# Key and value projections of an RWKV-7/GLA decoder trunk in plain float32, with the first group's scores and inversion placed later

## The chip, the cores and the metric

The kernel runs on one core of one Trainium2 chip. The metric is the device time of one execution in microseconds (us), median of several runs, lower is better. The engines are named as in the profile: PE (TensorE, matmuls; PEld is its weight load), DVE (VectorE), ACT (ScalarE), POOL (GpSimd) and SP, whose queue issues every DMA of this kernel.

## The reference

A two-layer decoder trunk on 272 tokens (16 learned meta tokens and 256 tokens of one sequence), width 2048, float32. Layer 0 mixes tokens by RWKV-7, layer 1 by gated linear attention; each is followed by a squared-ReLU MLP of width 8192. The change lies in layer 0:

```python
xx = jnp.pad(x, ((0, 0), (1, 0), (0, 0)))[:, :-1] - x
xr, xw, xk, xv, xa, xg = (x + xx * mix[i] for i in range(6))
r = xr @ w_rkv[0]
k = xk @ w_rkv[1]
v = xv @ w_rkv[2]
...
kk = hs(k * k_k)
kk = kk / jnp.maximum(jnp.sqrt(jnp.sum(kk * kk, axis=-1, keepdims=True)), 1e-12)
k = k * (1.0 + (a - 1.0) * k_a)
...
def step(S, inp):                     # 32 heads of 64
    r_t, w_t, k_t, v_t, a_t, b_t = inp
    sa = jnp.einsum('bhvk,bhk->bhv', S, a_t)
    S = S * w_t[:, :, None, :] + sa[..., None] * b_t[:, :, None, :] + v_t[..., None] * k_t[:, :, None, :]
    y = jnp.einsum('bhvk,bhk->bhv', S, r_t)
```

## The kernel before

Activations lie transposed: features on the 128 partitions, 272 tokens along the free dimension, so a vector of width 2048 is 16 tiles. A weight matrix is read in pieces of 128 x 1024 (512 KB, eight blocks of 128 x 128), two pieces for one output tile of 128 features.

**Products.** Most projections go through `proj`. `wload` loads a piece into one of three buffers `raw`, ScalarE rounds it into `hi` (L134) and VectorE forms the rest `lo = raw - hi` (L135), both of the type fp32r and with two buffers each. `mm3` then issues three matmuls for a block: hi by the high part of x (L140), hi by its low part (L141), lo by its high part (L142). The mixed inputs are split in the same way by `hl`. `proj32` is the other form: it loads a piece into `raw` and multiplies it as it is, in float32, with one matmul a block (L195), x being float32 too (`mix32`). Before the change it serves the three small projections (decay, learning rate, gate) alone.

**RWKV layer.** After the receptance projection comes the key stage, a loop over 16 output tiles f ("columns" here). A column projects k, in a PSUM bank of the ring `pj` for even f and of the ring `pt` for odd f (two banks each), loads `ca` (the decay sum and the learning rate, written earlier) by DMA, and forms on ScalarE and VectorE the scaled vectors `bk` and `ar`, which go to DRAM (`bkd`, `ard`). Two small matmuls per column sum over heads: L465 needs `sq`, L480 needs `kn`. At f = 3 the value input xv is mixed, at f = 4 the vectors of the first four columns (group 0 of four, eight heads each) are loaded back as BK and AR. At f = 6 all five token chunks of group 0 get their scores: `scores(0, c)` fills two `pt` banks with eight matmuls (L416) which VectorE evicts under a mask into AM. Then `invert(0)` is made: a generator of 52 steps on VectorE (transposes L431, L434, L445, L449, and 30 update pairs `upd`, `sysA`) that inverts the triangular 32 x 32 systems. From f = 8 on seven of its steps are issued per column.

The recurrence follows, group by group (g = 0 to 3), chunk by chunk (c = 0 to 4): `state` (L592) needs S of the chunk before, `solve` (L604), `emit`, which writes the new S on VectorE, `inner`, `turn`. Here the order on TensorE is written by hand: between the dependent steps `R(n)` runs n steps of a list of other products, one step being one 128 x 128 block. The list begins with the value projection (`v_proj`, 16 tiles of 16 blocks, 256 steps) and goes on with the output projection. 52 steps run before `merge(0)` (L535, L545), the counts in GAPS run inside the chunks, MARK gives the count reached before the merge of the next group (134, 214, 286). The scores and the inversion of group g+1 run inside group g; each merge waits for its inversion. `ahead` loads the next weight piece.

Elsewhere a scheduler of the language decides the order on each engine; DMA loads of weights have a raised priority. SP, like each engine, works its own list in order.

Of the kernel before, what the change touches and what calls it, by code (L numbers as in the profile page):

```python
# [17 lines left out]
P = 128  # L18
D = 2048
KT = D // P  # L20
NMETA = 16
SEQ = 256
T = NMETA + SEQ
# [30 lines left out]
class Kern:  # L54
# [130 lines left out]

    def proj32(self, srcs, x, n):
        nc = self.nc
        ps = self.pj()
        for i, s in enumerate(srcs):
            with self.tc.high_priority(offset=2000):  # L190
                raw = self.t(self.wp, [P, 1024], "raw", self.raw_bufs)
                nc.sync.dma_start(raw, s)
            for j in range(8):
                kt = 8 * i + j
                nc.tensor.matmul(ps[:, :n], raw[:, j * P : (j + 1) * P], x(kt), start=kt == 0, stop=kt == 8 * len(srcs) - 1)  # L195
        return ps[:, :n]
# [69 lines left out]
    def rwkv(self, done):  # L266
# [111 lines left out]
        for f in range(NR + 2, KT):  # L378
            nc.scalar.copy(rr[f], self.proj(pair(wr, f), xr, T))
            if f == NR + 2:  # L380
                for i in range(2):
                    nc.scalar.activation(gs[i], self.proj32(pair(lw, 2 + i), xg, T), AF.Sigmoid)
                xk = mix(2, ep)
            for i in range(3 if f < 14 else 2):
                lora(3 * (f - 10) + i if f < 14 else 12 + 2 * (f - 14) + i)
# [66 lines left out]
        for f in range(KT):  # L452
            r = rr[f]
            bk, ar = st2[0][f % 2], st2[1][f % 2]
            ps = self.proj(pair(wk, f), xk, T, bank=self.ptr if f % 2 else None)
            ca = self.t(ep, [P, 2, T], "ca", 2)
# [26 lines left out]
            if f == 3:  # L483
                xv = mix(3, self.xp)
                early2.close()
# [7 lines left out]
            if f == 4:  # L493
                load(0)
            if f == 6:
                for c in range(5):
                    scores(0, c)
                inv = invert(0)
            if f > 7:
                for _ in range(7):  # L500
                    next(inv, None)
# [171 lines left out]
        def units(x, n, ps):  # L673
            for i in range(n):
                hi, lo = weights.pop(0)
                for j in range(8):
# [4 lines left out]
                    if kt < 8 * n - 1:  # L681
                        yield

        def v_proj(f):
            ps = self.pj()[:, :T]
            yield from units(xv, 2, ps)
            nc.scalar.copy(hres[:, f], ps)
            tt(rr[f], rr[f], hres[:, f])
            yield
# [36 lines left out]
        def ahead():  # L726
            if srcs:
                weights.append(self.wload(srcs.pop(0)))
# [344 lines left out]
```

## Time and profile before

| | |
|---|---|
| three runs, median (lowest to highest) | 2659.4 us (2648.26 to 2670.31) |
| profiled execution | 2651.93 us, span 2649.9 us, mean granted clock 0.986 |
| instructions in the span | 47706 |
| PE, PEld | 96%, 89% busy |
| DVE, ACT, POOL | 64%, 47%, 0% busy |
| DMA | 450.17 MB, mean 170 GB/s |
| chain that ended last | 77% PE, 3% DVE, 1% ACT |
| key stage in the trace | about 167 to 332 us, up to the first merge |
| recurrence up to the merge of group 3 | about 332 to 582 us |

A busy PE is not a PE at its peak: a matmul shows about 0.29 us where the next one starts 0.125 us later. So prices of matmuls are read here from the starts of neighbouring rows. Rows name the line, engine, operation and the tiles written and read; `[1.86 <-ACT sq L462]` at the end of a row is the idle time before it and what ended it.

### The profile page before, as it was taken

How to read it: one execution, taken by the hardware profiler on the slowest of the kernel's cores; microseconds unless marked ns; L12 is line 12 of the kernel's file. 1: busy time of each engine (PE TensorE's matmuls, PEld its weight loads, DVE VectorE, ACT ScalarE, POOL GpSimd, SP SyncE). 2: the span in 40 equal slices, each digit the busy share in tenths (PEclk: the TensorE clock that was granted, in tenths of full speed). 3: DMA queues.
4: the chain of work that ended last, by engine and by line, in shares of the span. 5: the costliest groups of instructions: out<-in, count | busy, mean ns of one | idle time of the engine just before them, and what ended most of it. 6: DMA issues, size and time to landing. Idle time of an engine off the chain costs nothing.

```text
span 2649.9 us, 47706 instructions
## 1 busy us (share of the span) xinstructions
PE 2551.9 (96%) x19492; PEld 2364.2 (89%) x19492; DVE 1688.0 (64%) x2794; ACT 1257.3 (47%) x2011; POOL 10.8 (0%) x35
## 2 busy tenths in 40 slices
PE   7998988888999999999999999999999999999998
PEld 7887977777999999999999999998888888888887
DVE  8677976775755545545545666676766656656665
ACT  5364644445544434434434544454555535435444
POOL 0000000000000000000000000000000000000000
PEclk9998999989999999999999999999999999999999
DMA  5565732322455555555555544444555555555554
GB/s 192 180 217 205 245 137 85 100 79 93 160 174 176 175 175 175 176 176 178 177 177 176 176 150 148 155 167 144 188 186 189 186 189 189 186 189 189 186 190 159
DMA packets 137083, 450.17 MB, mean 170 GB/s; under 512 B 15760, under 2 KB 23696, under 8 KB 136864
## 3 DMA queue, kind: packets, MB, share of 16 engines
q1 hardware_dynamic: 136864, 447.12, 49.3%
q8 instruction: 153, 2.51, 0.4%
q14 instruction: 66, 0.54, 0.1%
HBM read 431.07 MB, written 15.99 MB: 169 GB/s over the span
## 4 chain that ended last, share of the span: by engine, by line
PE 77%; DVE 3%; ACT 1%; issue 0%; DVEq 0%; ACTq 0%
PE pj L168 23%; PE pj L140 13%; PE pj L142 13%; PE pj L141 13%; PE pj L169 12%; DVE lo L135 1%; PE pt L908 1%; PE pm L657 0%; PE pu L917 0%; DVE upd L268 0%; PE pt L897 0%; DVE sysA L268 0%; PE pm L648 0%; PE pm L558 0%; PE pt L416 0%
## 5 line engine op out<-in xcount | busy, mean ns | idle before, releaser
L134 ACT CAST hi<-raw 128x1024 fp32r<-128x1024 f32 (+1 forms) x834 | 813.6, 983 | 1086.7 <-PE pj L141 566.8
L135 DVE TENSOR_TENSOR lo<-raw,hi 128x1024 fp32r<-128x1024 f32 (+1 forms) x834 | 946.8, 1142 | 596.6 <-ACT hi L134 583.6
L140 PE MATMUL pj<-x,hi 128*128 128x272 f32 x2224 | 657.0, 296 | 6.6 <-ACT x L308 4.1
L142 PE MATMUL pj<-x,lo 128*128 128x272 f32 x2224 | 645.1, 290 | 0.2 <-DVE lo L135 0.2
L141 PE MATMUL pj<-x,hi 128*128 128x272 f32 x2224 | 643.4, 289 | 0.0
L168 PE MATMUL pj<-x,hi 128*128 128x512 f32 x1664 | 587.6, 396 | 0.6 <-DVE x L827 0.6
L169 PE MATMUL pj<-x,lo 128*128 128x256 f32 x1664 | 468.6, 282 | 1.3 <-DVE lo L135 1.3
L140 PEld LDWEIGHTS pj<-x,hi 128*128 128x128 f32 x2224 | 421.4, 190 | 15.1 <-ACT x L308 4.9
L141 PEld LDWEIGHTS pj<-x,hi 128*128 128x128 f32 x2224 | 424.2, 191 | 2.0
L142 PEld LDWEIGHTS pj<-x,lo 128*128 128x128 f32 x2224 | 420.7, 189 | 1.6 <-DVE lo L135 0.7
L168 PEld LDWEIGHTS pj<-x,hi 128*128 128x128 f32 x1664 | 313.2, 188 | 76.3 <-issue 2.9
L168 PE MATMUL pj<-h,hi 128*128 128x512 f32 x1024 | 358.5, 394 | 0.0
L169 PEld LDWEIGHTS pj<-x,lo 128*128 128x128 f32 x1664 | 314.1, 189 | 2.8 <-DVE lo L135 1.9
L140 PE MATMUL pj<-h,hi 128*128 128x272 f32 x1024 | 294.7, 288 | 0.0
L142 PE MATMUL pj<-h,lo 128*128 128x272 f32 x1024 | 293.9, 287 | 0.0
L141 PE MATMUL pj<-h,hi 128*128 128x272 f32 x1024 | 293.5, 287 | 0.0
L169 PE MATMUL pj<-h,lo 128*128 128x256 f32 x1024 | 288.5, 282 | 0.0
L168 PEld LDWEIGHTS pj<-h,hi 128*128 128x128 f32 x1024 | 192.4, 188 | 44.3
L141 PEld LDWEIGHTS pj<-h,hi 128*128 128x128 f32 x1024 | 193.7, 189 | 0.0
L169 PEld LDWEIGHTS pj<-h,lo 128*128 128x128 f32 x1024 | 193.5, 189 | 0.0
L140 PEld LDWEIGHTS pj<-h,hi 128*128 128x128 f32 x1024 | 192.6, 188 | 0.0
L142 PEld LDWEIGHTS pj<-h,lo 128*128 128x128 f32 x1024 | 192.1, 188 | 0.0
(246 smaller groups left out, 2223.1 us busy)
## 6 DMA issues: line engine op xcount, KB each, us to landing
raw<-mlp_w_d SPq DMA_DIRECT2D x512, 512.0 KB, 3.2
raw<-gla_in_d SPq DMA_DIRECT2D x98, 512.0 KB, 3.2
raw<-w_rkv_d SPq DMA_DIRECT2D x80, 512.0 KB, 3.7
raw<-gla_o_d SPq DMA_DIRECT2D x32, 512.0 KB, 3.2
raw<-w_r_d SPq DMA_DIRECT2D x16, 512.0 KB, 3.3
raw<-rw_oA_d SPq DMA_DIRECT2D x16, 512.0 KB, 3.3
raw<-rw_oB_d SPq DMA_DIRECT2D x16, 512.0 KB, 3.2
ard<-ar SPq DMA_DIRECT2D x16, 288.0 KB, 3.7
```

The lines of the kernel that those rows point to most:

```text
L134: nc.scalar.copy(hi[:, h], raw[:, h])
L135: nc.vector.tensor_tensor(out=lo[:, h], in0=raw[:, h], in1=hi[:, h].bitcast(F32), op=ALU.subtract)
L140: nc.tensor.matmul(out, hi[:, ws], xh, start=first, stop=False)
L141: nc.tensor.matmul(out, hi[:, ws], xl, start=False, stop=False)
L142: nc.tensor.matmul(out, lo[:, ws], xh, start=False, stop=last)
L168: nc.tensor.matmul(wide, hi[:, ws], x[kt][:, :, off : off + SEQ], start=kt == 0, stop=False)
L169: nc.tensor.matmul(ps[:, :SEQ], lo[:, ws], x[kt][:, 0, off : off + SEQ], start=False, stop=kt == nk - 1)
L908: nc.tensor.matmul(pa[:w, i * C : (i + 1) * C], KX[i][:, dt, s * P : s * P + w], Q[:, dt, i * C : (i + 1) * C], start=dt == 0, stop=dt == 1)
```

## The change

The key projection and the value projection use plain float32: xk and xv are mixed without a split, k goes through `proj32`, which gets the argument `bank`, and `v_proj` multiplies raw pieces itself, `ahead` loading the 32 pieces of the value weights without the split. The output projection stays as it was. Of group 0, chunk c of the scores is issued at column 6 + c instead of all five at column 6; the inversion is made at column 10, and its steps are issued eleven per column from column 11 on, instead of seven from column 8. Lines up to L494 keep their numbers; the value matmul is L693 afterwards, its load L739.

```diff
-    def proj32(self, srcs, x, n):
+    def proj32(self, srcs, x, n, bank=None):
         nc = self.nc
-        ps = self.pj()
+        ps = bank() if bank else self.pj()
...
-                xk = mix(2, ep)
+                xk = mix32(2, ep)
...
-            ps = self.proj(pair(wk, f), xk, T, bank=self.ptr if f % 2 else None)
+            ps = self.proj32(pair(wk, f), xk, T, bank=self.ptr if f % 2 else None)
...
-                xv = mix(3, self.xp)
+                xv = mix32(3, self.xp)
...
-            if f == 6:
-                for c in range(5):
-                    scores(0, c)
+            if 5 < f < 11:
+                scores(0, f - 6)
+            if f == 10:
                 inv = invert(0)
-            if f > 7:
-                for _ in range(7):
+            if f > 10:
+                for _ in range(11):
                     next(inv, None)
...
         def v_proj(f):
             ps = self.pj()[:, :T]
-            yield from units(xv, 2, ps)
+            for i in range(2):
+                w = weights.pop(0)
+                for j in range(8):
+                    if j == 3:
+                        ahead()
+                    kt = 8 * i + j
+                    nc.tensor.matmul(ps, w[:, j * P : (j + 1) * P], xv(kt), start=kt == 0, stop=kt == KT - 1)
+                    if kt < KT - 1:
+                        yield
...
         def ahead():
-            if srcs:
+            if len(srcs) > len(order) - 4 - KT:
+                with tc.high_priority(offset=2000):
+                    raw = self.t(self.wp, [P, 1024], "raw", self.raw_bufs)
+                    nc.sync.dma_start(raw, srcs.pop(0))
+                weights.append(raw)
+            elif srcs:
                 weights.append(self.wload(srcs.pop(0)))
```

How the scheduler moves instructions, at three places. First TensorE where the scores of group 0 begin; `pj_2391` is k of column 6, `pt_2546` of column 7, the other `pt` tiles are score banks. Before:

```order
L142 MATMUL pj_2391<-x_1151,lo_2425 128x272
L465 MATMUL pm_2463<-sq_2456,cst_117 128x272
L416 MATMUL pt_2486<-AR_433_2194,BK_432_2193 128x128
L416 MATMUL pt_2487<-AR_433_2194,BK_432_2193 128x128
...
L416 MATMUL pt_2534<-AR_433_2194,BK_432_2193 64x64 x4
L416 MATMUL pt_2535<-AR_433_2194,BK_432_2193 64x64 x4
L140 MATMUL pt_2546<-x_1136,hi_2549 128x272
```

and now, with `pj_2039` k of column 6, `pt_2106` of column 7, `kn_2010` of column 5 and `kn_2065` of column 6:

```order
L195 MATMUL pj_2039<-x_1143,raw_2050 128x272 x2
L416 MATMUL pt_2094<-AR_369_1922,BK_368_1921 128x128 x4
L416 MATMUL pt_2095<-AR_369_1922,BK_368_1921 128x128 x4
L195 MATMUL pt_2106<-x_1136,raw_2107 128x272 x2
L195 MATMUL pt_2106<-x_1137,raw_2107 128x272 x2
L480 MATMUL pm_2035<-kn_2010,cst_117 128x272
L465 MATMUL pm_2071<-sq_2064,cst_117 128x272
L195 MATMUL pt_2106<-x_1138,raw_2107 128x272 x2
```

Where all five chunks stood between columns 6 and 7, one chunk stands there now, and L480 of column 5 comes behind it.

Second, VectorE during the inversion: `sysA` and `upd` are its steps, `lo` a split of a weight piece, `kn`, `kk`, `bk`, `ar` the vectors of a column. Before (column 8):

```order
L135 TENSOR_TENSOR lo_2778<-raw_2775,hi_2777 128x1024
L268 TENSOR_TENSOR kn_2707<-pj_2641,kn_2707 128x272
L268 TENSOR_TENSOR upd_2959<-sysA_2197 128x184
L268 TENSOR_TENSOR bk_1719<-kn_2707,iW_2704 128x4x64
L268 TENSOR_TENSOR bk_1719<-kn_2707,iW_2704 128x16
L469 SCALAR_TENSOR_TENSOR kk_2705<-sq_2706,kk_2705 128x272
L476 SCALAR_TENSOR_TENSOR kn_2707<-r_15_89,vecs_119,kn_2707 128x272
```

and now (column 11):

```order
L268 TENSOR_TENSOR sysA_1925<-sysA_1925,upd_2517 128x23x8
L268 TENSOR_TENSOR kn_2400<-pt_2374,kn_2400 128x272
L268 TENSOR_TENSOR upd_2520<-sysA_1925 128x198
L268 TENSOR_TENSOR bk_1664<-kn_2400,iW_2397 128x4x64
L268 TENSOR_TENSOR bk_1664<-kn_2400,iW_2397 128x16
L268 TENSOR_TENSOR sysA_1925<-sysA_1925,upd_2520 128x22x9
L476 SCALAR_TENSOR_TENSOR kn_2400<-r_18_92,vecs_119,kn_2400 128x272
L268 TENSOR_TENSOR upd_2523<-sysA_1925 128x210
```

The splits are gone, and a step of the inversion stands between most instructions of a column.

Third, SP at the weight loads of column 7 and the loads of `ca`. Before (`raw_2547` and `raw_2577` are the pieces of column 7, `ca_2357` is column 5's):

```order
L478 DMA ard_80<-ar_1722 128x576
L475 DMA bkd_79<-bk_1720 128x576
L457 DMA ca_2357<-cad_78 128x544
L128 DMA raw_2547<-w_rkv_d 128x1024
L401 DMA BK_432_2193<-bkd_79 128x4x576
L128 DMA raw_2577<-w_rkv_d 128x1024
```

and now (`raw_2107` and `raw_2117` are the pieces of column 7, `ca_2005` is column 5's, `ca_2060` column 6's):

```order
L475 DMA bkd_79<-bk_1663 128x576
L401 DMA BK_368_1921<-bkd_79 128x4x576
L192 DMA raw_2107<-w_rkv_d 128x1024
L192 DMA raw_2117<-w_rkv_d 128x1024
L457 DMA ca_2005<-cad_78 128x544
L457 DMA ca_2060<-cad_78 128x544
```

The load of column 5's `ca` stood ahead of both pieces of column 7 and stands behind them now.

## The prediction

> **What bounds the kernel now.** I read the page's busy table first, then the busy time by stage, then the waits of the stages that the change touches, and last single rows of TensorE for prices. The line of busy times:
>
> ```profile
> PE 2551.9 (96%) x19492; PEld 2364.2 (89%) x19492; DVE 1688.0 (64%) x2794; ACT 1257.3 (47%) x2011; POOL 10.8 (0%) x35
> ```
>
> TensorE sets the pace of the whole, but the change touches only the stretch from the key projection to the third merge of the recurrence. Busy time there by stage; the columns are the stage, its length, busy us of PE, PEld, DVE, ACT and POOL with their instructions, granted clock, DMA share and GB/s:
>
> ```profile
> 167.00:332.00 165.00, 151.85 (x1079) 141.56 (x1080) 145.08 (x386) 97.78 (x193) 2.06 (x3) 0.94 0.68 228
> 332.00:409.00 77.00, 65.26 (x1004) 59.70 (x1000) 58.19 (x134) 31.84 (x72) 1.63 (x3) 0.93 0.38 129
> 409.00:494.00 85.00, 73.51 (x1022) 64.34 (x1016) 62.82 (x144) 37.43 (x85) 1.63 (x3) 0.94 0.30 100
> 494.00:582.00 88.00, 70.71 (x1006) 61.64 (x1008) 67.44 (x157) 38.38 (x89) 1.63 (x3) 0.93 0.26 82
> ```
>
> The first row holds the 16 columns of the key projection and 52 steps of the value projection, the other three the recurrence of groups 0 to 2 up to the merge of the next. TensorE is idle for 13.1, 11.7, 11.5 and 17.3 us, 53.7 us in all, and a clock of 0.93 or 0.94 over 415 us is worth another 27 us. So about 80 us are lost there, and a change that adds TensorE work can be paid from them. What TensorE waits for (us in all, times, longest), in the key stage:
>
> ```profile
> PE pm L465 <- ACT sq L462: 4.3, 5, 1.9
> PE pm L480 <- DVE kn L476: 3.1, 4, 1.4
> PE pt L416 <- DMA AR<-ard: 2.8, 1, 2.8
> PE pt L416 <- DVE AM L268: 2.6, 4, 1.1
> ```
>
> in group 0:
>
> ```profile
> PE pu L592 <- DVE upd L268: 5.0, 1, 5.0
> PE pu L592 <- DVE S L268: 4.5, 2, 3.3
> ```
>
> in group 1:
>
> ```profile
> PE pu L592 <- DVE S L268: 5.0, 2, 2.8
> PE pm L648 <- DVE hres L658: 3.3, 2, 2.4
> ```
>
> and in group 2:
>
> ```profile
> PE pt L535 <- DVE sysA L445: 6.5, 2, 6.3
> PE pu L592 <- DVE S L268: 4.2, 2, 2.9
> ```
>
> All but the AR load end on VectorE or ScalarE, the two engines that the change relieves.
>
> **Price of one weight block.** TensorE just before, in and just after the gate projections, which are plain float32 already; the columns are start and duration in us:
>
> ```profile
> 75.73 0.29 PE L140 MATMUL pj<-x,hi 128*128 128x272 f32 x1
> ...
> 79.87 14.83 PE L195 MATMUL pj<-x,raw 128*128 128x272 f32 x64
> 94.33 0.49 PE L140 MATMUL pj<-x,hi 128*128 128x272 f32 x1
> ```
>
> From 75.73 to the L195 row stand 33 matmuls of the three-product form: (79.87-75.73)/33 = 0.1255 us each, 0.376 us for the three of one 128x128 block. The 64 records of L195 are two output tiles of 16 blocks, two records a block: (94.33-79.87)/32 = 0.452 us. A block costs 0.0755 us more in plain float32. The Trainium skill ("FP8 and Floating Point Precision", TensorE Precision Notes) says that true FP32 takes four passes through the array; at the 0.1255 us of a pass here that would be 0.502 us a block and +64 us over the 512 blocks. The L195 row decides against the size, not the sign: it is 0.452, and the sum goes by that.
>
> **Key projection, 16 columns of 16 blocks.** Grouped rows of the stretch 167 to 332 (count, then busy us, mean ns and idle time before):
>
> ```profile
> L140 PE MATMUL pj<-x,hi 128*128 128x272 f32 x178 | 52.6, 295 | 0.0
> L140 PE MATMUL pt<-x,hi 128*128 128x272 f32 x128 | 38.9, 304 | 0.0
> L135 DVE TENSOR_TENSOR lo<-raw,hi 128x1024 fp32r<-128x1024 f32 (+1 forms) x47 | 48.2, 1040 | 5.2 <-ACT hi L134 5.0
> L268 DVE TENSOR_TENSOR x<-xm,x 128x272 fp32r<-128x272 f32 x10 | 4.2, 431 | 0.3 <-ACT x L308 0.2
> L268 DVE TENSOR_TENSOR upd<-sysA 128x30 f32<-128x30 f32 (+14 forms) x30 | 9.8, 327 | 0.3
> L268 DVE TENSOR_TENSOR sysA<-sysA,upd 128x30 f32<-128x30 f32 (+14 forms) x30 | 9.8, 327 | 0.3
> L449 DVE STREAM_TRANSPOSE AM<-sysA 32x256 f32<-32x256 f32 x8 | 4.7, 622 | 0.1
> L431 DVE STREAM_TRANSPOSE sysA<-AM 32x256 f32<-32x256 f32 x8 | 4.4, 594 | 0.1
> L445 DVE STREAM_TRANSPOSE sysA<-sysA 32x256 f32<-32x256 f32 x4 | 2.4, 646 | 0.1
> ```
>
> 178+128 = 306 blocks (key, and the first of value) gain 0.0755 us: **+23.1 us**. VectorE loses 48.2 + 4.2 of its 145.1 us, and ScalarE the cast hi<-raw that stands ahead of each lo. So the two small waits of a column (L465 for sq, L480 for kn) should shrink. The casts of the mixed inputs go too; those of xk stood beside TensorE work before 167 and I cost them at nothing; were that cover gone it would be a gain of 16 x 0.431 = 6.9 us of VectorE.
>
> The lump of the first group's scores is what can be won back. TensorE around it:
>
> ```profile
> 218.10 0.29 PE L142 MATMUL pj<-x,lo 128*128 128x272 f32 x1
> 220.24 0.73 PE L465 MATMUL pm<-sq,cst 128*128 128x272 f32 x2 [1.86 <-ACT sq L462]
> 223.78 2.08 PE L416 MATMUL pt<-AR,BK 64*128 64x128 f32 x16 [2.81 <-DMA AR<-ard]
> ...
> 238.18 1.71 PE L416 MATMUL pt<-AR,BK 64*64 64x64 f32 x16 [0.37 <-DVE AM L268]
> 239.82 0.59 PE L140 MATMUL pt<-x,hi 128*128 128x272 f32 x1
> ```
>
> Its clock, in slices of 10 us (0.62, 0.50 and 0.86 after the wait, 1.00 ahead of it):
>
> ```profile
> 220.00:230.00 10.00, 5.82 (x35) 4.83 (x36) 3.42 (x6) 2.75 (x8) 0.00 (x0) 0.62 0.72 274
> 230.00:240.00 10.00, 8.57 (x51) 6.94 (x51) 6.75 (x23) 2.08 (x5) 0.00 (x0) 0.50 0.26 88
> 240.00:250.00 10.00, 9.80 (x66) 9.55 (x66) 9.46 (x23) 2.92 (x4) 0.16 (x1) 0.86 0.12 39
> ```
>
> From 218.2 to 239.8 pass 21.6 us. In them lie four chunks at 2.08, the short one at half of 1.71 (its clock was half), and L465 and L480 at 0.45 each: 10.1 us of work, 11.5 lost, and 0.14 x 10 = 1.4 more after 239.8: **12.9 us lost**. The Trainium skill ("TensorE: Matmul & The Clock Gate", Part 1) says that an idle window of some 3.4 us halves the clock; the rows agree. By it the cold spell goes with the lump, unless a new wait is as long.
>
> What comes in its place. The work of the stage was 306 x 0.376 = 115.1, the 64 records of L465 and L480 at 0.226 (two a matmul, as for L195) = 14.5, scores 9.2, the other 17 of the 1079 records about 2.2: 141.0 of 165, so 24.0 lost, 12.9 in the lump and 11.1 elsewhere. A column is 16 x 0.452 + 4 x 0.226 = 8.1 us after the change. After: one chunk a column means that its two banks and the odd columns' bank come from the same ring of two. Chunk 0 needs the bank of column 5, which frees when kn of column 5 is formed, and that column's ca load now stands on SP behind two weight loads whose buffers TensorE must free first: rows for the landings are
>
> ```profile
> raw<-w_rkv_d SPq DMA_DIRECT2D x36, 512.0 KB, 4.0
> ca<-cad SPq DMA_DIRECT2D x16, 272.0 KB, 4.0
> ```
>
> That ca load is released 4.1 us into column 6 (8 blocks and a record pair) and lands some 5 later; with 2 us on ScalarE and VectorE the bank is free 11 us in, where TensorE stands after 8.7 (column, one record pair, half a chunk): 2.3 us. The other four chunks I take at 0.8 each, half of the 1.86 us that L465 waited in the lump: 5.5. Columns 0 to 5 lose 0.3 each: 1.8. In columns 10 to 15 the whole inversion runs: 9.8+9.8+4.7+4.4+2.4 plus two transposes at 0.6 = 32.3 us of VectorE, beside (145.1-48.2-4.2-32.3)/16 = 3.8 a column: 55 us against 6 x 8.1 + 2.1 = 51 of TensorE. The surplus of 4 fits into the 52 value blocks behind (23.5 us, hardly any VectorE work), so I keep 0.6 a column, about what the 16 columns lost outside the lump (11.1/16): 3.6. Lost after: 5.5+1.8+3.6 = 10.9. The stage goes from 165 to 141.0+23.1+10.9 = 175.0: **+10.0**. Bounds: 4 lost (+3.1) and all 24.0 lost again (+23.1).
>
> **Weight loads.** A load now waits until TensorE has read the buffer, no longer for the split on VectorE. Behind it on SP stand the ca load and the bk and ar stores; who waits for those is L459 and then L480. Three buffers of 8 blocks give 2 x 3.6 = 7.2 us of lead against 4.0 of landing: nothing added but the 2.3 counted above.
>
> **Recurrence.** Blocks of value in groups 0, 1, 2: 82, 80, 42 (204 of the 256 less 52), +6.2, +6.0, +3.2. Where nothing else delays S, the wait for it is
>
> ```profile
> 620.81 0.24 PE L592 MATMUL pu<-S,AR 64*64 64x64 f32 x1 [1.11 <-DVE S L268]
> ```
>
> 1.11 us. I let the S waits fall to it, since between two of them VectorE had one or two splits (1.04 us in the row of lo) that go. Group 0: 4.5-2x1.11 = 2.2, 1.0 of the 5.0 for upd (transposes, which stay), 1.0 of the cold clock: net +2.0. Group 1: 2.8, 1.5 of hres (the longer wait falls to the shorter, 3.3-2.4), 1.0: +0.7. Group 2: 2.0, 1.5 as in group 1, and 4.0 of the 6.3 for sysA, as four splits of 1.04 leave a queue that is full up to the merge: -4.3. Sum **-1.6**; bounds -8 (double the relief) and +7 (half of it).
>
> **Sum.** +10.0 - 1.6 = +8.4 us. The profiled execution took 2651.9 us, 2.0 more than its span: 2660. The median of the three runs is 2659.4, 7.5 higher, and would give 2668; I set 2666, from a base of 2657.6 between the two.
>
> **Rivals.** (a) Relief pays fully: 4 us lost in the key stage and -8 in the recurrence, 3.1-8 = -5: 2653. For it: the waits named end on the relieved engines. Against: the columns' waits were only 7.4 us. To come 1% (27 us; that is about what a measurement of this kernel tells from no change) below the median, 38.5 + 27 of the 80 lost us would have to go. (b) Slower: the bank ring and a bunched inversion make VectorE the bound in columns 6 to 15. L480 and the second half of each chunk stand in TensorE's order behind VectorE's kn. For it: 55 against 51 us above. Against: 48 us of splits have gone. Each us that VectorE hands kn late costs ten; from 1.9 a column on it is +19 on top, 2685, just over 1%. (c) Nothing is given back: 510 blocks x 0.0755 = +38.5, 2696. Against: the lump's 12.9 us have a visible cause, and it is spread. (d) A block costs four passes of 0.1255 each: 512 x 0.1255 = 64 in place of 38.5, 2666+25.5 = 2692. The page named above has this rule; the L195 row, 0.452 over 32 blocks, is against it.
>
> **Chances.** Forecast 0.55; (a) 0.15 and beyond 1% 0.07; (b) 0.16, of which 0.09 beyond 1%; (c) 0.06; (d) 0.01. Faster by over 1% 0.07, slower 0.16, the rest 0.77. The range goes from -5 and the low base (2644) to (b) with a margin for the spread of the runs before, 2648 to 2670: 2692.
>
> **What would show it.** Key records at 0.226 us start to start; no gap over 2.5 us and a clock of 1.00 between columns 5 and 10; the stretch up to the first merge 175 us long, not 165; S waits near 1.1; the wait of the third merge for sysA near 2. Wrong it would be if L480 waits 2 us or more for kn in most of columns 10 to 15, if L195 waits for raw loads, or if the cold spell moves elsewhere.

## The result: 0.9% slower, and the profile after

The changed kernel took a median of 2682.3 us over 8 runs (2678.3 to 2691.8), the kernel before 2656.6 over 8 runs beside it (2648.3 to 2670.3). The ratio is 1.0093, with a 95% interval of 1.0073 to 1.0113: 25.7 us slower, within the 1% that the prediction called no change, and within its range of 2644 to 2692. The forecast of 2666 was 16 us too low. Medians here and below leave out single executions in a far slower state, one of e1 and one of e12.

The profiled execution took 2689.7 us for a span of 2687.9, 38.0 more than the one of before. The line of busy times after:

```profile
PE 2596.7 (97%) x18980; PEld 2361.7 (88%) x18980; DVE 1607.3 (60%) x2666; ACT 1183.3 (44%) x1883; POOL 10.8 (0%) x35
```

VectorE has 80.7 us less to do and ScalarE 74.0, TensorE 44.8 us more. Busy time by stage, in the columns of the prediction's table; the rows are the key stage, groups 0 to 2 of the recurrence, and all that follows the recurrence:

```profile
166.00:347.40 181.40, 171.91 (x762) 136.68 (x762) 99.45 (x323) 58.80 (x135) 2.07 (x3) 0.98 0.64 216
347.40:432.20 84.80, 72.68 (x909) 58.64 (x908) 46.86 (x113) 20.93 (x52) 1.62 (x3) 0.92 0.29 95
432.20:527.10 94.90, 81.43 (x947) 63.16 (x946) 54.33 (x129) 27.99 (x69) 1.62 (x3) 0.93 0.29 93
527.10:612.60 85.50, 73.50 (x960) 59.29 (x959) 60.23 (x140) 32.82 (x77) 1.62 (x3) 0.94 0.24 76
...
667.00:2688.00 2021.00, 2004.34 (x13671) 1867.87 (x13664) 1212.20 (x1711) 937.76 (x1353) 2.46 (x12) 1.00 0.53 174
```

The key stage went from 165.0 to 181.4 us, group 0 from 77 to 84.8, group 1 from 85 to 94.9, and group 2 from 88 to 85.5. In the key stage TensorE now idles 9.5 us instead of 13.1, at a clock of 0.98 instead of 0.94; in groups 0 and 1 it idles a little more than before (12.1 and 13.5 us against 11.7 and 11.5), at about the same low clock. The last row is work that the change doesn't touch. In the execution of before it took

```profile
640.00:2650.00 2010.00, 1993.37 (x13645) 1856.36 (x13643) 1211.83 (x1709) 937.45 (x1352) 2.46 (x12) 1.00 0.51 175
```

and the window of before opens 1.4 us behind the last record of L592, that of after 0.1. From that record to the end it is 2011.4 us before and 2021.0 after, so about 10 of the 38 us lie in work that is the same in both; the last section returns to it. For this reason I compare the kernels below by their medians and by stages, not by span.

What TensorE waits for after the change (us in all, times, longest), in the key stage:

```profile
PE pm L480 <- DVE kn L476: 5.9, 4, 2.7
PE pm L465 <- ACT sq L462: 1.6, 3, 1.0
PE pt L195 <- DVE kn L268: 0.9, 1, 0.9
PE pt L416 <- DVE AM L268: 0.8, 1, 0.8
PE pj L195 <- DMA raw<-w_rkv_d: 0.2, 1, 0.2
```

in group 0:

```profile
PE pu L592 <- DVE S L268: 5.8, 2, 5.2
PE pu L592 <- DVE upd L268: 5.0, 1, 5.0
```

and in groups 1 and 2, for S alone:

```profile
PE pu L592 <- DVE S L268: 6.9, 3, 3.1
...
PE pu L592 <- DVE S L268: 5.5, 3, 4.3
```

The lump's wait for AR is gone, the third merge no longer waits for sysA (6.3 us before), and a load is waited for only 0.2 us. But the waits for S, which the prediction let fall to 1.1 us each, have grown in every group: 4.5, 5.0 and 4.2 us before, 5.8, 6.9 and 5.5 after. (The 5.0 us put down to upd are the same before and after. They are a wait for S too: L592 reads S and AR, and a step that writes upd starts while S is being written.)

The rows that show what S stands behind are on VectorE, ahead of the longest of them. In the kernel before, the product pu of the same chunk was ready at 388.9 us, and a split and steps of the inversion came ahead of the update of S:

```profile
390.13 0.39 DVE L268 TENSOR_TENSOR upd<-sysA 128x220 f32<-128x220 f32 x1
390.44 1.28 DVE L135 TENSOR_TENSOR lo<-raw,hi 128x512 fp32r<-128x512 f32 x2
391.64 0.38 DVE L268 TENSOR_TENSOR sysA<-sysA,upd 128x220 f32<-128x220 f32 x1
392.05 0.42 DVE L268 TENSOR_TENSOR S<-pu,S 128x256 f32<-128x256 f32 x1
```

After the change, VectorE's last rows before that update, and TensorE's row behind it:

```profile
410.17 0.19 DVE L268 TENSOR_TENSOR sysA<-sysA,upd 128x30 f32<-128x30 f32 x1
410.40 2.08 DVE L445 STREAM_TRANSPOSE sysA<-sysA 32x256 f32<-32x256 f32 x4
412.50 0.42 DVE L268 TENSOR_TENSOR S<-pu,S 128x256 f32<-128x256 f32 x1
412.96 0.60 DVE L449 STREAM_TRANSPOSE AM<-sysA 32x256 f32<-32x256 f32 x1
413.58 0.42 DVE L268 TENSOR_TENSOR S<-S,WC 128x256 f32<-128x256 f32 x1
```

```profile
414.16 0.28 PE L592 MATMUL pu<-S,AR 64*32 64x64 f32 x1 [5.15 <-DVE S L268]
```

Now pu was ready at 408.0, and not one split stands here. VectorE runs the next group's inversion without a gap, and the update of S comes after 2.1 us of elimination steps and four transposes of 2.1 us together. The splits were taken out, and S stands behind more of the inversion than before. Where TensorE idles so long, its clock falls, to 0.66 in this slice of 10 us:

```profile
410.00:420.00 10.00, 5.84 (x62) 4.92 (x63) 6.00 (x13) 0.79 (x2) 0.00 (x0) 0.66 0.08 18
```

The price of a block can now be read over a long undisturbed run of value matmuls (start and length in us, count; and of the same 72 records the mean length of one in ns):

```profile
329.62 16.66 PE L693 MATMUL pj<-x,raw 128*128 128x272 f32 x72
```

```profile
L693 PE MATMUL pj<-x,raw 128*128 128x272 f32 x72 | 16.7, 392 | 0.0
```

From the first start to the last lie (16.66 - 0.39)/71 = 0.2292 us a record, 0.4583 a block. Against 3 x 0.1255 = 0.3765 a block costs 0.082 us more, not the 0.0755 of the prediction, and the 512 blocks 41.9 us.

### The profile page after: what moved, and what is told of

Its sections match the earlier page's. It is cut to its first block, busy times and chain, and to the rows that moved or that the text cites. A ratio compares the mean times of both kernels' runs of the same rounds, so it can differ in the third digit from the quotient of the medians.

```text
span 2687.9 us, 46307 instructions
## 1 busy us (share of the span) xinstructions
PE 2596.7 (97%) x18980; PEld 2361.7 (88%) x18980; DVE 1607.3 (60%) x2666; ACT 1183.3 (44%) x1883; POOL 10.8 (0%) x35
## 4 chain that ended last, share of the span: by engine, by line
PE 89%; DVE 7%; DMA 2%; ACT 1%; issue 1%; SPq 0%; DVEq 0%; ACTq 0%
PE pj L168 23%; PE pj L140 13%; PE pj L141 13%; PE pj L142 13%; PE pj L169 12%; PE pj L693 4%; PE pj L195 2%; DVE sysA L268 1%; DVE upd L268 1%; DMA ca<-cad 1%; PE pt L195 1%; PE pt L416 1%; DVE lo L135 1%; PE pt L922 1%; DVE AM L449 0%
## 5 line engine op out<-in xcount | busy, mean ns | idle before, releaser
L135 DVE TENSOR_TENSOR lo<-raw,hi 128x1024 fp32r<-128x1024 f32 (+1 forms) x738 | 866.3, 1178 | 588.8 <-ACT hi L134 576.0
L134 ACT CAST hi<-raw 128x1024 fp32r<-128x1024 f32 (+1 forms) x738 | 743.3, 1011 | 1053.9 <-PE pj L141 543.9
L140 PE MATMUL pj<-x,hi 128*128 128x272 f32 x1840 | 539.1, 293 | 6.6 <-ACT x L308 4.1
L142 PE MATMUL pj<-x,lo 128*128 128x272 f32 x1840 | 531.4, 289 | 0.0
L141 PE MATMUL pj<-x,hi 128*128 128x272 f32 x1840 | 531.2, 289 | 0.0
L168 PEld LDWEIGHTS pj<-x,hi 128*128 128x128 f32 x1664 | 312.4, 188 | 76.4 <-issue 2.9
L140 PEld LDWEIGHTS pj<-x,hi 128*128 128x128 f32 x1840 | 345.8, 188 | 11.1 <-ACT x L308 4.9
L141 PEld LDWEIGHTS pj<-x,hi 128*128 128x128 f32 x1840 | 349.9, 190 | 1.1
L142 PEld LDWEIGHTS pj<-x,lo 128*128 128x128 f32 x1840 | 347.2, 189 | 0.4
L169 PEld LDWEIGHTS pj<-x,lo 128*128 128x128 f32 x1664 | 313.2, 188 | 2.8 <-DVE lo L135 1.9
```

The source lines that it names most:

```text
L134: nc.scalar.copy(hi[:, h], raw[:, h])
L135: nc.vector.tensor_tensor(out=lo[:, h], in0=raw[:, h], in1=hi[:, h].bitcast(F32), op=ALU.subtract)
L140: nc.tensor.matmul(out, hi[:, ws], xh, start=first, stop=False)
L141: nc.tensor.matmul(out, hi[:, ws], xl, start=False, stop=False)
L142: nc.tensor.matmul(out, lo[:, ws], xh, start=False, stop=last)
L168: nc.tensor.matmul(wide, hi[:, ws], x[kt][:, :, off : off + SEQ], start=kt == 0, stop=False)
```

## The experiments

All times of stages are from profiled executions, read from the first record of L465 to the first record of L535 of merge 0 (key), from there to merge 1, 2 and 3 (groups 0 to 2), and to the last record of L592 (group 3). Ratios are to the kernel before, run beside each. In e5 the first columns run ahead of the mark, so its first two figures don't compare.

| kernel | median us | ratio, 95% interval | key | group 0 | group 1 | group 2 | group 3 |
|---|---|---|---|---|---|---|---|
| before | 2656.6 | | 155.1 | 77.0 | 85.4 | 87.7 | 56.7 |
| after | 2682.3 | 1.0093 (1.0073 to 1.0113) | 171.7 | 84.9 | 94.9 | 85.5 | 54.3 |
| e1 new places, three products | 2666.1 | 1.0034 (1.0009 to 1.0058) | 159.5 | 80.7 | 86.4 | 87.8 | 59.3 |
| e2 float32, old places | 2680.2 | 1.0086 (1.0054 to 1.0117) | 170.2 | 85.5 | 95.0 | 85.5 | 54.3 |
| e3 new places, key float32 | 2667.2 | 1.0044 (1.0016 to 1.0071) | 165.6 | 79.8 | 86.2 | 87.8 | 60.8 |
| e4 new places, value float32 | 2668.2 | 1.0034 (1.0010 to 1.0058) | 158.5 | 84.8 | 94.9 | 85.5 | 54.3 |
| e5 no splits, loads unpaced | 2692.8 | 1.0118 (1.0093 to 1.0142) | (137.5) | (75.4) | 84.9 | 81.0 | 60.7 |
| e6 after, S first | 2680.0 | 1.0075 (1.0049 to 1.0102) | 170.1 | 80.3 | 93.0 | 87.1 | 54.3 |
| e7 before, S first | 2654.5 | 0.9990 (0.9973 to 1.0007) | 152.8 | 75.5 | 85.6 | 87.9 | 56.7 |
| e8 before, lump a column later | 2653.5 | 0.9974 (0.9956 to 0.9992) | 145.2 | 88.3 | 86.2 | 87.9 | 59.2 |
| e9 no splits, loads paced | 2645.3 | 0.9973 (0.9951 to 0.9994) | 148.9 | 76.9 | 85.3 | 85.1 | 56.3 |
| e10 after, no elimination steps | 2657.5 | 1.0002 (0.9986 to 1.0018) | 169.3 | 78.1 | 84.4 | 80.2 | 54.3 |
| e11 e8 and S first | 2649.3 | 0.9984 (0.9968 to 0.9999) | 144.8 | 81.1 | 87.5 | 87.9 | 56.7 |
| e12 after, steps spread | 2693.3 | 1.0124 (1.0102 to 1.0146) | 172.4 | 82.6 | 94.8 | 95.3 | 59.3 |

With float32 values the groups of after, e2 and e4 agree to 0.7 us. With values in three products group 0 lies between 75 and 81 (88 in e8) and group 3 between 56 and 61, and the granted clock goes with it: 0.93 in group 0 of before, 0.88 in e1, 0.89 in e3. A few us in those two columns say nothing. Each row of stages is one execution.

### The two halves of the change: e1 and e2

e1 adds to the kernel before only the new places; e2 takes them out of the changed kernel.

```diff
-            if f == 6:
-                for c in range(5):
-                    scores(0, c)
+            if 5 < f < 11:
+                scores(0, f - 6)
+            if f == 10:
                 inv = invert(0)
-            if f > 7:
-                for _ in range(7):
+            if f > 10:
+                for _ in range(11):
                     next(inv, None)
```

> The kernel before with only the second half of the change: scores one chunk per column in columns 6 to 10, inversion from column 11 on, all weights still in three products. Theory A (price and placement simply add; what VectorE and ScalarE are relieved of buys nothing): the lump's waits and cold clock go, the chunks fall from 17.4 us to 10.6 as they did after the change, and the waits of L480 for kn rise by up to 6: 2650 to 2657 us, so the new place is a small gain by itself. Theory B (the float32 form pays for the new place): with two splits of 1.04 us a column still on VectorE, columns 11 to 15 have 32.3/5 + 3.8 + 2.1 = 12.4 us of VectorE against 6.9 of TensorE; the surplus of 27 us is covered only in part by the 52 value blocks (19.6 us): 2665 to 2672, with waits of L480 for kn of 3 us or more a column.

> The changed kernel with only the first half of the change: key and value in plain float32, scores in one lump after column 6 and the inversion from column 8 on, as before. Theory A: the lump costs again what the trace of before shows (chunks 17.4 us instead of 10.6), the waits for kn fall from 5.9 to about 3: 2682 + 7 - 3 = 2686 us. Theory B: relieved of splits, VectorE and ScalarE shorten the lump's own waits (sq, AM) and the bunching of the inversion is gone: 2680 or less.

The new places alone made the kernel slower by 0.34%, as theory B had it, but not where B looked. What TensorE waits for in the key stage of e1:

```profile
PE pt L535 <- DVE sysA L445: 8.5, 1, 8.5
...
PE pt L416 <- DMA AR<-ard: 3.0, 1, 3.0
...
PE pm L480 <- DVE kn L476: 0.3, 1, 0.3
```

L480 hardly waits for kn. Instead the first merge waits 8.5 us for the last transposes of the inversion. And the wait for AR is still there: spreading the chunks didn't remove it. In e2, float32 with the lump in its old place, there is no such wait, and the slices in which before had a clock of 0.62, 0.50 and 0.86 read

```profile
220.00:230.00 10.00, 8.51 (x44) 6.79 (x42) 2.43 (x8) 3.59 (x9) 0.00 (x0) 1.00 0.91 333
230.00:240.00 10.00, 9.98 (x51) 7.84 (x52) 8.19 (x31) 3.58 (x9) 0.00 (x0) 0.83 0.35 120
240.00:250.00 10.00, 10.00 (x65) 7.99 (x64) 8.38 (x17) 0.94 (x2) 0.16 (x1) 1.00 0.47 144
```

So it is the float32 columns, 8.4 to 8.6 us each ahead of the lump instead of 6.6 to 8.4, that bring TensorE there late enough: in e2 AR and BK have both landed by 224.6 us, and the first record of L416 starts at 226.2 without a wait, at 223.8 before with one. The medians of e2 and the changed kernel, 2680.2 and 2682.3, can't be told apart. In the key stage the new places cost 4.4 us with three products and 1.5 with float32; that fits theory B's interaction, which is small, as far as one execution of each can show it.

### Key alone and value alone: e3 and e4

Both keep the new places. e3 has the value projection back in three products, e4 the key projection (each undoes the diff's lines for the other).

```diff
-                xv = mix32(3, self.xp)
+                xv = mix(3, self.xp)
```
```diff
-            ps = self.proj32(pair(wk, f), xk, T, bank=self.ptr if f % 2 else None)
+            ps = self.proj(pair(wk, f), xk, T, bank=self.ptr if f % 2 else None)
```

> The changed kernel with the value projection back in three products; key float32, new places of scores and inversion kept. Theory A: value loses 256 blocks x 0.082 us = 21, times the 1.13 by which blocks in the recurrence take longer than at full clock = 23.7: 2658 us, and the waits for S stay at 4 to 6 us a group. Theory B: the relief of VectorE in the recurrence had paid part of that back, so less is won: 2665 or more, with longer waits for S than the changed kernel has (5.8, 6.9, 5.5 us in groups 0 to 2).

> The changed kernel with the key projection back in three products; value float32, new places of scores and inversion kept. Theory A: 256 blocks x 0.082 us = 21 are won: 2661 us. Theory B: VectorE, with two splits a column and the inversion in columns 11 to 15, becomes the bound there, and part or all of the 21 us is lost again in waits of L480 for kn: 2668 to 2680.

Both medians, 2667 and 2668, lie on the side of theory B: taking either projection back wins 14 to 15 us, not 21 to 24. Against e1, key alone costs nothing that the medians can tell (2667.2 against 2666.1), and value alone as little (2668.2), while both together cost 16. The stages say how. Float32 keys on top of e1 add 6.1 us to the key stage, for some 240 blocks behind the first L465 whose price is 20: most comes back there. Float32 values lengthen groups 0 and 1 (from 79.8 and 86.2 in e3 to 84.9 and 94.9 in the changed kernel; from 77.0 and 85.4 against before), and give back in groups 2 and 3, where the wait of the third merge for sysA ends; e3 still has it, 5.6 us.

In the recurrence, e4 and the changed kernel are the same to 0.1 us. So the whole change there is the value projection's. The longer waits for S that theory B put into e3 didn't come: they are 4.7, 6.6 and 4.8 us in groups 0 to 2, a little less than after the change. Nor did the waits of L480 for kn that theory B put into e4: they are 1.3 us in all, and the longest wait of its key stage is 4.5 us for the load of BK. So both times are theory B's, and its reasons are not shown.

### What the relief alone is worth: e5 and e9

To see the relief without the price, both multiply every key and value block with one tile that was rounded ahead of column 0, in three products, with the places of e1.

```diff
-            hi, lo = self.wload(s)
+            hi, lo, *raw = (load or self.wload)(s)
             for j in range(8):
...
+                if raw and j == 7:
+                    self.nc.tensor.matmul(ps[:, :1], raw[0][:, j * P : (j + 1) * P], xt[:, 0, :1].bitcast(F32), start=False, stop=False)
```

> Relief alone. The kernel of e1 (new places, three products), but key and value blocks multiply with one weight tile that was rounded once ahead of column 0: the 64 casts hi<-raw and the 64 splits lo<-raw of the key and value weights are left out (so keys and values are not those of the reference); their weights are still loaded, and one element a row is copied on GpSimd. TensorE's work is that of before. Theory A (relief buys nothing): the stages of e1 again, 159.5 us from the first L465 to the first merge, then 80.7, 86.4 and 87.8; 2667 us. Theory B (relief pays, and float32 costs its full price of 0.082 us a block besides): the difference between price and cost is won without the price: 25.2 - 12.2 = 13 us in the key stage (146 us), 3 in group 0, nothing in group 1, 6 in group 2 (the wait of the merge for sysA) and 3 in group 3: 2642 us. In both the waits for S in groups 0 and 1 stay, since what stands ahead of S on VectorE is the inversion.

> e5 once more with its loads paced: a weight tile is now read by TensorE (one column of its last block, accumulated in plain float32) and not by GpSimd, so that a load waits for TensorE as in the changed kernel. Left out as in e5: the casts and splits of the key and value weights, and the weights themselves; 64 one-column matmuls are added, whose cost the trace shows. Theory A (relief buys nothing): 159.5 us from the first L465 to the first merge, 80.7, 86.4 and 87.8 for groups 0 to 2, as in e1; 2667 us. Theory B (relief pays 13 us in the key stage, and in the recurrence only where the merge waits for sysA): about 147, 77 to 81, 85 to 86, and 82; 2645 us.

e5 failed as an experiment. With nothing but a copy of one column on GpSimd to hold a load back, the weight loads ran ahead of everything else on SP's queue, and one small load that TensorE needs waited behind them:

```profile
PE pm L376 <- DMA l<-lora_d: 44.0, 1, 44.0
```

e9 paces the loads by TensorE and answers the question. Its rows for the key stage and groups 0 to 2:

```profile
178.00:327.00 149.00, 145.56 (x1081) 136.89 (x1081) 97.25 (x320) 54.92 (x129) 2.09 (x3) 1.00 0.73 243
327.00:404.00 77.00, 67.73 (x1013) 62.30 (x1011) 46.68 (x113) 20.95 (x52) 1.62 (x3) 0.93 0.34 118
404.00:489.00 85.00, 75.07 (x1044) 66.20 (x1043) 52.79 (x125) 26.54 (x65) 1.62 (x3) 0.94 0.31 102
489.00:574.00 85.00, 71.89 (x1016) 62.74 (x1014) 59.23 (x142) 34.53 (x81) 1.62 (x3) 0.93 0.28 89
```

VectorE and ScalarE do about what they do after the change (97, 47, 53 and 59 us of VectorE), TensorE what it did before. The key stage is 148.9 us against 159.5 in e1, although the added one-column matmuls take 5.1 of it (72 records, 0.07 us from each to the next start): relief is worth 10.6 us there, and 15.7 if the added matmuls cost all of their time. The clock is 1.00.

In the recurrence, where the places are those of before, groups 0 and 1 take what they took before (76.9 and 85.3 against 77.0 and 85.4), with 11.5 and 10.0 us less on VectorE. Yet the waits for S fell, from 4.5, 5.0 and 4.2 us before to these in groups 0, 1 and 2:

```profile
PE pu L604 <- DVE S L276: 2.9, 2, 2.2
...
PE pu L604 <- DVE S L276: 3.4, 2, 2.4
...
PE pu L604 <- DVE S L276: 2.7, 2, 2.2
```

That is about 1.6 us a group, and in groups 0 and 1 the added matmuls take it up (20 records, 1.65 us from start to start in each). Group 2, with 12 such records, wins 2.6; its merge waits 4.2 us for sysA instead of 6.3. So splits were part of what S waited behind: at the four longer waits of before, 1.4 to 1.6 us of splits and 1.3 to 2.0 us of steps lie between the end of pu and S. Theory B holds within 2 us in the key stage and groups 0 and 1; for group 2 it had 82 us, and the trace shows 85.1.

e9 and the changed kernel leave VectorE the same work in the recurrence, and their waits for S differ by 2.8 to 3.5 us a group. What differs there is above all TensorE's value blocks: e4, with float32 values alone, has the groups of the changed kernel, and e3, with values in three products, does not. Why the planner that sets VectorE's order puts more steps ahead of S beside float32 blocks was not tested.

The pieces of the key stage add up to 159.5 (e1) - 15.7 + 292 blocks behind the mark x 0.082 = 167.7 us; the changed kernel has 171.7, so 4 us of it have no cause here, unless part of the 5.1 us of the added matmuls filled time that was idle in e1.

### What holds S: e6, e7, e10 and e12

e6 and e7 give the update of S priority in the planner, in the changed kernel and in the one before; TensorE's order stays.

```diff
+                with tc.high_priority(offset=40):
                     if c:
                         tt(sb, pS, sb, ALU.add)
                         src = sb
                     tt(sb, src, WC[:, 4 * g : 4 * g + 4, c : c + 1].to_broadcast([P, 4, HEAD]))
```

> The changed kernel; in the recurrence the two VectorE instructions that update S are given priority over the inversion's steps, nothing else (TensorE's order is the same). Theory A (the waits for S are an order on VectorE: the inversion's steps stand ahead of S): the waits of 5.0, 5.2, 3.1, 3.1 and 4.3 us of L592 fall to 1.1 each, 15 us, and with the cold clock behind them 15 to 19: group 0 from 84.9 to 76, group 1 from 94.9 to 90, group 2 from 85.5 to 82; 2665 us. Theory B (VectorE has no time left there): the inversion ends later by as much and the merges wait for sysA instead; 2678 to 2684.

> The kernel before, with the same priority for the update of S. Theory A: the waits of 5.0, 3.3, 2.8, 2.2 and 2.9 us fall to 1.1 each, 10.7 us, in part paid back in group 2, whose merge waits 6.3 us for sysA already and would wait longer: 2657 - 7 = 2650. Theory B: splits and inversion fill VectorE, and the merges wait for sysA by as much as S is earlier: 2657.

Neither median moved by more than the intervals allow (2680.0 against 2682.3; 2654.5, ratio 0.9990 with 1 in its interval). In e6 groups 0 and 1 got 4.6 and 1.9 us shorter and group 2 1.6 longer. The priority did not always move S up: the three waits of group 0 went from 5.0, 0.6 and 5.2 us to 1.6, 3.8 and 1.5, and in group 1 two of 3.1 and 2.6 us remained, with steps of the inversion still ahead. So e6 doesn't separate the theories. e10 does, by taking the steps away.

```diff
             for s in range(1, 31):
+                if g:
+                    yield
+                    continue
                 n, m = 31 - s, s
```

> The changed kernel, with the 30 elimination steps of the inversion (60 VectorE instructions, upd and sysA) left out for groups 1 to 3; the transposes, the merges and group 0's inversion stay, and the output is not the reference's. Theory A (TensorE waits for S because the elimination steps stand ahead of S on VectorE, splits or no splits): in groups 0 to 2 the waits of 5.2, 3.1, 3.1 and 4.3 us fall to 1.1 each, 11.3 us, with some 3 of cold clock; the 5.0 for upd, behind ten transposes, stays. Groups 84.9, 94.9, 85.5 go to about 79, 90, 81; 2668 us. Theory B (the waits for S are the chain of S itself, through uv, pu and rs, or TensorE's price alone makes the groups longer): the groups stay within 2 us, 2680.

```profile
351.00:429.00 78.00, 71.62 (x917) 57.70 (x910) 26.58 (x53) 20.83 (x52) 1.62 (x3) 0.96 0.31 103
429.00:513.00 84.00, 76.74 (x941) 59.76 (x934) 34.07 (x69) 28.00 (x69) 1.62 (x3) 0.98 0.33 104
513.00:593.00 80.00, 71.94 (x958) 57.79 (x958) 40.96 (x80) 32.83 (x77) 1.62 (x3) 0.96 0.27 86
```

With 20 us less on VectorE in each group (26.6, 34.1 and 41.0 against 46.9, 54.3 and 60.2), the groups are 6.8, 10.5 and 5.3 us shorter, and the median is 24.8 us below that of the changed kernel. Theory A is confirmed, with 22.6 us where it forecast 14. In group 0 the wait of 5.0 behind the transposes stays, as forecast; in group 1 this is all that is left of the wait for S, and in group 2 it is the same:

```profile
PE pu L595 <- DVE S L268: 0.7, 1, 0.7
```

and the clock of group 1 is up from 0.93 to 0.98. Where the steps had been, VectorE now starts the update of S 0.05 us behind the end of pu (411.02 and 411.07 us in group 0). So in the changed kernel S waits behind the elimination steps. e10 takes twice as much off VectorE as e9 did, so the lengths of the groups alone would not tell the order from the load.

e12 asks whether the order alone is to blame: no work is left out, but the steps keep the order of the code, and five instead of nine stand at each place, so that many run beside the value blocks ahead of a merge.

```diff
-                tt(w, X[:, s + 1 :, s : s + 1].to_broadcast([P, n, m]), X[:, s : s + 1, :m].to_broadcast([P, n, m]))
+                i = tt(w, X[:, s + 1 :, s : s + 1].to_broadcast([P, n, m]), X[:, s : s + 1, :m].to_broadcast([P, n, m]))
+                if g:
+                    tc.keep_in_program_order(i)
...
-                    some(inv, 9)
+                    some(inv, 5)
```

> The changed kernel, with the elimination steps of groups 1 to 3 kept on VectorE in the order of the code and five, not nine, at each place, so that the last 17 calls run beside the value blocks ahead of the merge, where VectorE stood nearly idle; no work is left out. Theory A (TensorE waits for S because steps that are due later stand ahead of it): part of the 22.6 us that e10 won by leaving the steps out comes back, 10 to 16 us: 2666 to 2672, with waits for S of 2 us or less and no wait of the merges over 2. Theory B (VectorE has to do these steps somewhere on the path, and what S gains the merges lose): 2678 to 2685, with waits of L535 for sysA.

The waits for S fell: to 5.3 us in all in group 0 (10.8 with the one for upd before the edit), 3.1 in group 1, 3.6 in group 2. But the three merges behind these groups now wait for the inversion, the last for long:

```profile
PE pt L537 <- DVE sysA L447: 3.9, 1, 3.9
...
PE pt L537 <- DVE sysA L447: 3.9, 1, 3.9
...
PE pt L537 <- DVE sysA L447: 9.2, 1, 9.2
```

It is 11.0 us slower than the changed kernel, 8 more than theory B had at most: what S gained the merges lost, for this spread. A spread between five and nine, or another one for each group, wasn't tried.

### The lump's loss: e8 and e11

```diff
-            if f == 6:
+            if f == 7:
                 for c in range(5):
                     scores(0, c)
```

> The kernel before, with the lump of the first group's scores and the start of its inversion one column later (after column 7, inversion steps from column 8 on as before). It tells apart what made the lump's loss: Theory A (the AR load that had not landed, 2.8 us, and the cold clock behind that wait): one column (7 us) later it has landed, so the wait and the cold spell of some 9 us go: 2648 us, and the clock of the lump is 1.0. Theory B (the lump itself: sq, AM and the banks): the loss moves with it, 2657.

> The kernel before (three products) with the lump one column later, as e8, and the priority for S, as e7. Theory A (the two gains add: 0.26% and 0.1%): 2650 us or less, ratio 0.9965. Theory B (both only move a wait to the merges and the clock of group 0): ratio 0.998 to 1.0, as e7 and e8 alone.

In e8 the first record of L416 starts without a wait at 225.5 us, and the slices read

```profile
220.00:230.00 10.00, 10.00 (x72) 9.02 (x72) 5.28 (x6) 4.50 (x8) 0.00 (x0) 1.00 0.99 350
230.00:240.00 10.00, 10.00 (x68) 8.41 (x69) 7.25 (x24) 6.70 (x14) 0.00 (x0) 1.00 0.63 209
240.00:250.00 10.00, 9.21 (x60) 7.95 (x59) 9.65 (x29) 2.37 (x6) 0.00 (x0) 0.83 0.47 145
```

The key stage is 9.9 us shorter, as theory A had it: AR landed at 223.7 us, as before, and TensorE came later. But the edit did more than that. Seven products of column 8 now stand behind each of the first three banks of scores, so that the lump is no lump any more, and the wait for sq (1.9 us) ahead of AR's is gone too, and most of those for AM (0.6 us left of 2.6). e8 doesn't tell these apart. e2 kept the lump, without the waits for AR and sq, and there those for AM are 0.8 us.

In this one execution group 0 then took 11.3 us longer, at a clock of 0.88, from two short waits of the merge on (1.2 and 1.6 us for ScalarE's copies); the median of 12 runs still says that 0.26% was won, between the two theories. Moving one number by one wins some 7 us over the kernel before, where the change to float32 lost 26. e11, with S first on top of it, is at 0.9984: the two gains don't add. Both are faster than either kernel of the case, by little.

## Why the prediction was right, point by point, and where it was not

The sign, the range and "within 1%" were right, and the reason that carried them too: the price of float32 is paid in full by TensorE, and only part of it is given back. Too small was the sum: +8.4 us forecast, 25.7 measured between the medians. That this still lies inside the range is in part luck, since the range reaches to 2692 for rival (b), whose mechanism did not occur.

**Price of a block.** Mis-sized by 9%: 0.0755 forecast, 0.082 measured. The L195 row of before was divided from its start to the start of the next kind of matmul (14.46/32), and that next start comes 0.03 us behind the last record's own. Read by its own length the same row gives (14.83 - 0.39)/63 = 0.2292 a record, what the changed kernel has. Over 510 blocks that is 3.2 us. The Trainium skill ("TensorE: Matmul & The Clock Gate", Part 1) has a matmul start N / 2.4 GHz + about 2.5 ns behind the one ahead of it once the clock is up. If a record is two passes of 272 columns, with that 2.5 ns once, an estimate from this figure is 229.2 ns, and the trace agrees. By the same rule the estimate for a product of the three-product form is 115.8 ns, and here the trace shows 125.5: the three products are dearer than the rule, the four passes are not.

**Key stage, +10.0.** Measured +16.4 (165.0 to 181.4). The lost time was right in its size: named waits of 9.4 us against 10.9 forecast, L480's for kn 5.9 of them, with L480 above 2 us in two of the last columns and not in most. Missing were 1.9 us of price, 0.5 in the sum itself (half of 1.86 is 0.93 and not 0.8, four times), and the clock of 0.98, an estimated 0.02 x 171 = 3.4. The working behind the size was wrong in one step, that the cold spell goes with the lump: e1 spread the lump and kept the wait for AR, and lost 8.5 us at the merge as well. What removed that wait was the float32 columns' longer time (e2), as one column more does (e8). The forecast's givebacks were 12.9 - 5.5 for the lump and 11.1 - 5.4 in the columns, 13.1 us; e1 and e9 put -4.4 on the places and 10.6 to 15.7 on the relief, 6.2 to 11.3. The sum was near, by luck: the shares were not.

**Weight loads, nothing added.** Right: 0.2 us.

**Recurrence, -1.6.** This is the step that failed: "I let the S waits fall to it, since between two of them VectorE had one or two splits (1.04 us in the row of lo) that go." The three groups measured 7.9 + 9.5 - 2.2 = +15.2. The price there is 204 x 0.082 = 16.7 us (forecast 15.4). Of the 17.0 us of relief that the step let come back, 1.5 came, and that from one wait alone: the third merge's for sysA, 6.3 us, forecast to keep 2 and gone altogether. The waits for S and for hres did not fall. One or two splits did stand ahead of S, and where they went while TensorE's blocks stayed as they were (e9), its waits fell by about 1.6 us a group, less than the 2.0 to 2.8 forecast. In the changed kernel they rose, by 1.3 to 1.9 us a group, because elimination steps and transposes stood there instead; e10 shows this by leaving the steps out. The step of the prediction treated the splits as all that lay between pu and S, and let nothing move into their place. Its floor of 1.11 us was misread too: in that row of group 3 a split of 1.29 us stands ahead of S, and with the steps gone too (e10) all waits but one in each of groups 0 to 2 are 0.05 us or none. The bounds of that term, -8 to +7, didn't reach what came: they halved the relief, and didn't allow for none. (Nor is -8 "double the relief": twice 17.0 would give -18.6.)

**Rivals.** (a) fell: the relief paid in the key stage, and next to nothing in the recurrence of the changed kernel. (b) has the nearest time, 2685, and the wrong mechanism: L480's waits for kn were 5.9 us in all and not 19. The inversion on VectorE is what TensorE waits for in the recurrence, which (b) left out. (c), nothing given back, is exceeded in groups 0 and 1, which got 17.4 us longer for 162 x 0.082 = 13.3 us of price; the whole gave some back: of 41.9 us of price, 25.7 were left. (d) fell: 0.458 and not 0.502 a block.

**What would show it.** A stretch to the first merge of 181 us and not 175, and waits for S of up to 5.2 us and not 1.1. Between columns 5 and 10 no gap was over 2.5 us, but the clock was 0.85 from 230 to 240. The three signs that the prediction named against itself hardly came: L480 waited 2 us or more for kn twice, not in most of columns 10 to 15, L195 waited 0.2 us for one load, and the clock of the recurrence, 0.92, 0.93 and 0.94 by groups, had been 0.93, 0.94 and 0.93 before.

## What to carry to other kernels

Relief of an engine pays only if nothing else moves into its place: look at the rows that stand directly ahead of the releaser, since other work may come to stand where some was taken out, and the wait may be for that. Price such a change with the added work in full, and count a wait as gone only if everything between the input's arrival and the releaser is what you remove. Before restructuring, try to move the consumer of a late load by one step: here that edit of one number won 0.26%, and the change lost 0.9%.

## What the runs showed of the hardware that was not expected

The same matmuls ran at two paces in different executions, both at a granted clock of 1.00. From 100 to 800 us behind the recurrence, the mean from start to start was 0.125 us in the profiled executions of before, e2 and e4, and 0.127 in those of after and e1; the other nine ran at 0.125. Over those 700 us that makes 10 us, the difference behind the recurrence named above, with no wait to explain it; what sets the pace is open.

The clock falls with less idleness than one long wait. In e8, the three slices of 3 us around the first merge's two waits:

```profile
326.00:329.00 3.00, 1.84 (x33) 1.62 (x33) 2.97 (x8) 2.62 (x6) 0.00 (x0) 1.00 0.98 315
329.00:332.00 3.00, 1.41 (x57) 1.24 (x50) 1.04 (x2) 1.66 (x6) 0.00 (x0) 0.88 0.57 186
332.00:335.00 3.00, 3.00 (x15) 3.00 (x16) 0.00 (x0) 0.57 (x2) 0.00 (x0) 0.55 0.86 263
```

TensorE was busy for 3.25 of the first 6 us, no single wait was longer than 1.6, and the clock went to 0.55 in the slice behind. It is 1.00 in the stretch from 327.89 to 331.30, in which TensorE was busy for 1.04 of 3.41 us, and 0.50 in the next one as long. The Trainium skill ("TensorE: Matmul & The Clock Gate", Part 1) speaks of an idle window of about 3.4 us; here a partly busy one sufficed. So it did in the lump, whose rows the prediction took to agree with that: no wait there is longer than 2.81 us, and L465 runs between it and the wait of 1.86 ahead.

Loads that little holds back can keep a small one from being issued, because SP works its list in order. In e5 SP issued 41 weight loads, then at 228.6 us the load of lora_d that stood behind them; it landed at 234.4, and TensorE had stood still for 44.0 us:

```profile
157.50 68.41 SPq L141 DMA_DIRECT2D raw<-w_rkv_d  x41
...
228.58 1.35 SPq L373 DMA_DIRECT2D l<-lora_d  x2
```

The weight loads moved some 300 GB/s meanwhile:

```profile
200.00:220.00 20.00, 0.00 (x0) 0.00 (x0) 0.00 (x0) 0.00 (x0) 2.01 (x11) 0.50 0.91 302
```
